# Hyena's inverse transforms turned round: the table stationary, 256 channels moving, results with times on partitions

## The chip, the cores and the metric

One core of a Trainium2 chip. The time is the device time of one execution in microseconds; the kernel before was run three times, and the median counts. The trace comes from one more execution, which was profiled.

## What is computed

One layer of an encoder block over 512 tokens of 2048 features: a norm, a wide input projection, two branches (hyena, 1024 channels, and mlstm, four heads), a gated merge, and a feed-forward part of 5632 hidden units. The change lies in hyena: for each channel, two long convolutions by FFT of length 1024, each with a bias term, between three short-convolved inputs hv, hx1, hx2.

```python
filt = hyena_filters(L, ...)                      # (512, order, 2, 1024)
kf = two_sided_spectrum(filt)                     # h_fwd, one zero, h_bwd reversed without its time 0
z = hx1 * long_conv(hv, kf[:, 0], hb[0])
y_a = hx2 * long_conv(z, kf[:, 1], hb[1])

def long_conv(u, kf, bias):
    uf = jnp.fft.rfft(u, n=2 * L, axis=1)
    y = jnp.fft.irfft(uf * kf[None], n=2 * L, axis=1)[:, :L]
    return y + u * bias
```

## The kernel before

**Numbers.** Every large product is made of three float32r matmuls (`mm3`, L72): each operand is split into a high part, a cast on ScalarE, and a low part, a subtraction on VectorE (`gsplit` L316 with its operations at L319 and L320, `split_w` L165 with L169 and L170). `mm` is L70, so all of these matmuls carry that line; in the trace the moving operand is named first and the stationary one second. Small products in plain fp32 also go through `mm`.

**Main work and side work.** The input projection (`w_in_cols`, L1064) is the main generator. Each of its ticks is two blocks of contraction: 12 matmuls of 512 columns, or 24 of 256 for mlstm's v; there are 220 ticks. `Weights.get` (L180) emits the load (L162, SyncE's queue, three raw buffers) and the split of weights two units ahead of their use. In between, `drive` (L247) lets the side work go on: each tick gives it a budget of 2.2, and every `yield` of a side generator takes its cost from that. The side is two streams that take turns (`turns`, L900): one makes the filters' spectra, the other runs hyena for four groups q of 256 channels and mlstm for four heads, in the order hyena 0 and 1, mlstm 0, hyena 2 and 3, mlstm 1 to 3. A `yield "pause"` holds a stream back for two ticks; `need` waits for a result of the other. What is left of the side when the projection ends would run alone. Behind both comes the merge (a Winograd form, L985 on).

**Hyena for one q** (`hyena`, L743, `conv_long`, L680). Two tiles of u, each 128 channels by 512 times, are loaded by GpSimd's queue (L756 is the load of the gating tile x1 or x2). Times stand in four classes (every fourth time). Eight TensorE transposes (L688) into two PSUM tiles put times on the partitions, and `gsplit` splits them. The forward transform has the DFT table stationary (dH, dL) and 256 channels moving (`sums`, L576). The spectrum is multiplied with the filter's on VectorE and four sums of it are split (A). The inverse transform (L735 on) has the spectrum stationary, 128 channels of it, and 128 columns of the table moving; its result has channels on the partitions again. `finish` (L759) adds bias times u and multiplies by x1 (L764, into z) or by x2 (L768, which also reorders the times, and a store to d_ya, L769). For the second order z goes through transposes and split as u did.

**The filter's spectrum** (`spectrum`, L622). w3 comes by SyncE's queue, the window by GpSimd's (L633). Forward and backward filters are added and subtracted, so that at time 0 the sum holds the backward filter's first value too, which the reference leaves out. Two fp32 matmuls of w3 with `h2["c"]` (one column) give that value with channels on the partitions, and `hbias2` (L640) is the bias less that value.

**Buffers.** All tiles from `gt` and `vt` share 24 buffers (`NG`, L298), those of `sg` nine, the PSUM tiles of `sd_ps` four banks.

Of the kernel before, what the change touches and what calls it, by code (L numbers as in the profile page):

```python
# [9 lines left out]
F32R = mybir.dt.float32r  # L10
AF = mybir.ActivationFunctionType
# [4 lines left out]
P = 128  # L16
# [18 lines left out]
def hybrid_block_kernel(ctx, tc, x, norm1_w, w_in, conv_w, conv_b, filt_w1, filt_b1, filt_freq1,  # L35
# [6 lines left out]
    def new(pool, tag, shape=(P, L), dt=F32):  # L42
        n_tile[0] += 1
        return pool.tile(list(shape), dt, tag=tag, name=f"{tag}_{n_tile[0]}")
# [21 lines left out]
    def sd_ps():  # L66
        return new(psd, "sd")

    def mm(o, a, b, start, stop):
        nc.tensor.matmul(o, a, b, start=start, stop=stop)  # L70
# [20 lines left out]
    sel32 = csm[0:32, 3 * P:3 * P + 16]  # L91
    onesf = new(cp, "onesf", (P, P))
    nc.vector.memset(onesf, 1.0)
    onesr = new(cp, "onesr", (P, P), F32R)
    nc.vector.tensor_copy(onesr, onesf)

    xp_cm = tc.tile_pool(name="xp", bufs=1)
    xp = xp_cm.__enter__()
    rows_a = new(xp, "rows_a", (120, P))
    nc.scalar.dma_start(rows_a, conv_w[0].rearrange("k (b p) -> (k b) p", p=P))  # L100
    rows_b = new(xp, "rows_b", (88, P))
    nc.scalar.dma_start(rows_b[0:40], conv_b[0].rearrange("(b p) -> b p", p=P))
    nc.scalar.dma_start(rows_b[40:56], norm1_w[0].rearrange("(b p) -> b p", p=P))
    nc.scalar.dma_start(rows_b[56:72], norm2_w[0].rearrange("(b p) -> b p", p=P))
    nc.scalar.dma_start(rows_b[72:88], hyena_bias[0].rearrange("o (b p) -> (o b) p", p=P))
    cols = new(cp, "cols", (P, 208))
    pt = sd_ps()
    nc.tensor.transpose(pt[:, 0:120], rows_a, ident[0:120, 0:120])
    nc.tensor.transpose(pt[:, 120:208], rows_b, ident[0:88, 0:88])
    nc.vector.tensor_copy(cols, pt[:, 0:208])  # L110
    cw = cols[:, 0:120].rearrange("p (k b) -> p k b", k=3)
    cb = cols[:, 120:160]
    n1 = cols[:, 160:176]
    n2 = cols[:, 176:192]
    hbias = cols[:, 192:208]
    hbias2 = new(cp, "hbias2", (P, 16))


    def dram(name, shape=(P, L)):
# [188 lines left out]
    def sg(dt=F32, shape=(P, L)):  # L308
        n_tile[0] += 1
        return ph.tile(list(shape), dt, tag="sg", name=f"sg_{n_tile[0]}", bufs=9)  # L310
# [5 lines left out]
    def gsplit(src, shape=(P, L)):  # L316
        h = gt(F32R, shape)
        l = gt(F32R, shape)
        nc.scalar.copy(h, src)  # L319
        nc.vector.tensor_tensor(l, src, h.bitcast(F32), ALU.subtract)  # L320
        return h, l
# [192 lines left out]
    def filter_net():  # L514
        for m in range(4):
            t = gt()
            nc.gpsimd.dma_start(t, c_dft[m])
            hh = new(ph, f"dH{m}", dt=F32R)
            ll = new(ph, f"dL{m}", dt=F32R)
            nc.scalar.copy(hh, t)  # L520
            nc.vector.tensor_tensor(ll, t, hh.bitcast(F32), ALU.subtract)
            dft.append((hh, ll))
            yield 1
        vec = new(ph, "fvec", (P, 4))
        for j, src in enumerate((filt_b1, filt_freq1, filt_b2, filt_freq2)):
            for half in range(2):
                nc.gpsimd.dma_start(vec[half * 64:half * 64 + 64, j:j + 1], src[0].rearrange("(n o) -> n o", o=1))
        w1 = new(ph, "fw1", (33, 2, 64))
        w2 = new(ph, "fw2", (64, 2, 64))
        for half in range(2):  # L530
            nc.gpsimd.dma_start(w1[:, half, :], filt_w1[0])
            nc.gpsimd.dma_start(w2[:, half, :], filt_w2[0])
        zt = gt()
        nc.gpsimd.dma_start(zt[0:33], c_zt)

        def sin_layer(ps, b, fr):
            a = gt()
# [12 lines left out]
        yield 4  # L550
        h1 = sin_layer(ps, vec[:, 0:1], vec[:, 1:2])
        ps = sd_ps()
        mm(ps, w2.rearrange("p a b -> p (a b)"), h1[0:64], True, True)
        yield 4
        hh = sin_layer(ps, vec[:, 2:3], vec[:, 3:4])
        h2["H"] = new(ph, "h2H", dt=F32R)
        h2["L"] = new(ph, "h2L", dt=F32R)
        nc.scalar.copy(h2["H"], hh)
        nc.vector.tensor_tensor(h2["L"], hh, h2["H"].bitcast(F32), ALU.subtract)
        h2["c"] = new(ph, "h2c", (64, 1))  # L560
        nc.vector.tensor_copy(h2["c"], hh[0:64, 0:1])
        yield 4


# [57 lines left out]
    def spectrum(q, o):  # L622
# [8 lines left out]
        for b in range(2):  # L631
            t = gt(shape=(P, 2, 256))
            nc.gpsimd.dma_start(t, c_win[b * 256:(b + 1) * 256, c0:c0 + 256].rearrange("(b p) c -> p b c", p=P))  # L633
            wt.append(t)
        yield .1
        ps = sd_ps()
        for j in range(2):
            mm(ps[:, j:j + 1], w3[0:64, 256 + j * P:256 + (j + 1) * P], h2["c"], True, True)
        ci = o * 8 + 2 * q
        nc.vector.tensor_tensor(hbias2[:, ci:ci + 2], hbias[:, ci:ci + 2], ps[:, 0:2], ALU.subtract)  # L640
        wpm = gt()
        nc.vector.tensor_tensor(wpm[:, 0:256], w3[:, 0:256], w3[:, 256:512], ALU.add)
        nc.vector.tensor_tensor(wpm[:, 256:512], w3[:, 0:256], w3[:, 256:512], ALU.subtract)
# [6 lines left out]
        for tb in range(4):  # L650
            ts = slice(tb * P, (tb + 1) * P)
            ps = sd_ps()
            mm(ps, h2["H"][:, ts], stk, True, False)
            mm(ps, h2["L"][0:64, ts], stk[0:64], False, True)
            pq = gt()
            wv = wt[tb // 2][:, tb % 2:tb % 2 + 1, :].to_broadcast([P, 2, 256])
            nc.vector.tensor_tensor(pq.rearrange("p (j c) -> p j c", j=2), ps.rearrange("p (j c) -> p j c", j=2),
                                    wv, ALU.mult)
            h, l = sg(F32R), sg(F32R)
            nc.scalar.copy(h, pq)  # L660
            nc.vector.tensor_tensor(l, pq, h.bitcast(F32), ALU.subtract)
            PQ.append((h, l))
            yield 1.3
# [13 lines left out]
                yield "wait"  # L677
            yield from spectrum(n // 2, n % 2)

    def conv_long(q, o, u, finish):  # L680

        src = []
        for half in range(2):
            ps = sd_ps()
            for b in range(2):
                for j in range(2):
                    tc0 = half * 256 + b * P
                    nc.tensor.transpose(ps[:, b * 256 + j * P:b * 256 + (j + 1) * P], u[j][:, tc0:tc0 + P], ident)  # L688
            h, l = gsplit(ps)
            for b in range(2):  # L690
                src.append((h[:, b * 256:(b + 1) * 256], l[:, b * 256:(b + 1) * 256]))
            yield .6
        yield "pause"
        yield from need(("spec", q, o))
        U = []
# [33 lines left out]
                yield 1.2  # L729
        yield "pause"  # L730
        where = ((A[0], A[1]), (A[2], A[2]), (A[1], A[0]), (A[3], A[3]))
        for j in range(2):
            ps = sd_ps()
            for c in range(4):
                for sine in range(2):  # L735
                    yH, yL = where[c][sine]
                    dH, dL = table(1, c, sine)
                    cs = slice(sine * 256 + j * P, sine * 256 + (j + 1) * P)
                    mm3(ps[:, c * P:(c + 1) * P], yH[:, cs], yL[:, cs], dH, dL, sine == 0, sine == 1)
            finish(j, ps)  # L740
            yield 1.2

    def hyena(q):  # L743
        yield from need(("hy", q))
        u = []
        for j in range(2):
            t = gt()
            nc.gpsimd.dma_start(t, d_hy[0][2 * q + j])
            u.append(t)
        yield .1  # L750
        for o in range(2):
            nu = []
            xg = []
            for j in range(2):
                t = gt()
                nc.gpsimd.dma_start(t, d_hy[1 + o][2 * q + j])  # L756
                xg.append(t)

            def finish(j, ps):  # L759
                ci = o * 8 + 2 * q + j  # L760
                t = gt()
                nc.vector.scalar_tensor_tensor(t, u[j], hbias2[:, ci:ci + 1], ps, ALU.mult, ALU.add)
                if o == 0:
                    nc.vector.tensor_tensor(t, t, xg[j], ALU.mult)  # L764
                    nu.append(t)
                else:
                    y = gt()
                    nc.vector.tensor_tensor(natural(y), classes(t), classes(xg[j]), ALU.mult)  # L768
                    nc.gpsimd.dma_start(d_ya[2 * q + j], y)  # L769

            yield from conv_long(q, o, u, finish)
            u = nu
            yield "pause"


    def mlstm(h):
# [689 lines left out]
```

## Time and profile before

| | |
|---|---|
| median of 3 runs | 2948.95 us (2946.33 to 2950.16) |
| the profiled execution's own time | 2950.35 us |
| its span (first to last instruction) | 2948.6 us |
| TensorE busy, instructions | 2904.2 us, 18604 |
| VectorE busy, instructions | 2120.0 us, 3853 |
| ScalarE busy, instructions | 1259.9 us, 2234 |
| GpSimd busy, instructions | 187.7 us, 433 |

PE is TensorE's matmuls, PEld its loads of the stationary operand, DVE VectorE, ACT ScalarE, POOL GpSimd, SPq SyncE's DMA queue. A row names line, engine, operation, output and inputs by tile, shape and count, then busy time and mean duration of one, then the engine's idle time just before and what ended it. Busy time is that of a group's union, so overlapping matmuls count once, and the mean is one instruction's own duration, from start to modelled end. How far instructions follow each other is read from the timeline: start, duration, name, and how many were merged in the row.

### The profile page before, as it was taken

To read this page: it belongs to the slowest core of one execution; us is meant where nothing else is said; L and a number is where in the kernel's file an instruction comes from. 1 tells how busy PE (TensorE), PEld (TensorE's weight loads), DVE (VectorE), ACT (ScalarE), POOL (GpSimd) and SP (SyncE) were. 2 spreads that over 40 slices of the span, in tenths; PEclk is the share of its full clock that TensorE was granted. 3 is DMA by queue.
4 is the path that set the end of the run, shared out by engine and by line. 5 is a ranking of instruction groups with operands and counts; after the bars stand their busy time and mean duration, and the time that the engine had idled before them with its cause. 6 is when DMAs were issued, how large, how long until landed. Compare 5 with 4: busy or idle time off the path is not lost.

```text
span 2948.6 us, 48562 instructions
## 1 busy us (share of the span) xinstructions
PE 2904.2 (98%) x18604; PEld 2622.0 (89%) x18604; DVE 2120.0 (72%) x3853; ACT 1259.9 (43%) x2234; POOL 187.7 (6%) x433
## 2 busy tenths in 40 slices
PE   8999999999999999999999999999999999999998
PEld 6788887898779999888899999999999998888886
DVE  6889878878459888645447888888888885233336
ACT  5334343436535554423344444444444444333224
POOL 1001110101100000100010000000000000000000
PEclk9999999999999999999999999999999999999999
DMA  5333343333434444833444333343333436334433
GB/s 175 108 111 113 112 133 101 122 115 120 145 122 132 134 126 129 271 125 108 134 130 136 112 119 122 115 128 117 119 119 115 125 99 215 100 119 124 126 110 128
DMA packets 285201, 377.02 MB, mean 128 GB/s; under 512 B 18021, under 2 KB 221163, under 8 KB 284969
## 3 DMA queue, kind: packets, MB, share of 16 engines
q1 hardware_dynamic: 261264, 301.18, 33.2%
q0 software_dynamic: 22272, 70.55, 7.0%
q8 instruction: 145, 2.38, 0.3%
q10 hardware_dynamic: 1433, 2.20, 0.2%
q14 instruction: 87, 0.71, 0.1%
HBM read 326.67 MB, written 47.20 MB: 127 GB/s over the span
## 4 chain that ended last, share of the span: by engine, by line
PE 66%; issue 2%; DMA 2%; DVE 1%; ACT 0%; POOL 0%; SPq 0%; POOLq 0%; DVEq 0%; ACTq 0%
PE mm L70 46%; PE sd L70 20%; DMA wr<-in_w_down_dram 1%; DMA bt<-d_o 1%; PE sd L1225 0%; DMA d_o<-st 0%; DVE h L81 0%; DMA bt<-d_ya 0%; DVE T L1253 0%; DVE l L977 0%; DVE wl L170 0%; DVE s L993 0%; ACT h L80 0%; POOL d_o L390 0%; DVE x L1365 0%
## 5 line engine op out<-in xcount | busy, mean ns | idle before, releaser
L170 DVE TENSOR_TENSOR wl<-wr,wh 128x512 fp32r<-128x512 f32 x512 | 350.5, 689 | 489.1 <-ACT wh L169 483.7
L169 ACT CAST wh<-wr 128x512 fp32r<-128x512 f32 x512 | 316.4, 621 | 766.5 <-PE mm L70 725.7
L70 PE MATMUL mm<-a,wh 128*128 128x512 f32 (+1 forms) x2136 | 625.7, 376 | 0.9 <-ACT wh L169 0.8
L70 PE MATMUL mm<-T,h 128*128 128x256 f32 x2592 | 466.0, 282 | 3.9 <-ACT h L976 3.9
L70 PE MATMUL sd<-T,h 128*128 128x256 f32 x2592 | 463.8, 282 | 0.0
L70 PEld LDWEIGHTS mm<-a,wh 128*128 128x128 f32 x2136 | 387.0, 189 | 70.1 <-issue 2.6
L70 PEld LDWEIGHTS mm<-T,h 128*128 128x128 f32 x2592 | 400.6, 190 | 4.4 <-ACT h L976 4.4
L70 PE MATMUL mm<-a,wl 128*128 128x512 f32 (+1 forms) x1068 | 399.4, 375 | 3.4 <-DVE wl L170 3.3
L70 PEld LDWEIGHTS sd<-T,h 128*128 128x128 f32 x2592 | 399.4, 189 | 0.0
L70 PE MATMUL mm<-wh,h 128*128 128x512 f32 x1280 | 395.6, 390 | 3.0 <-ACT h L80 3.0
L70 PE MATMUL mm<-T,l 128*128 128x256 f32 x1296 | 366.0, 283 | 0.8 <-DVE l L977 0.8
L70 PE MATMUL sd<-T,l 128*128 128x256 f32 x1296 | 365.2, 282 | 0.0
L976 ACT CAST h<-s 128x512 fp32r<-128x512 f32 x395 | 244.5, 620 | 280.9 <-PE sd L70 138.3
L70 PEld LDWEIGHTS mm<-wh,h 128*128 128x128 f32 x1280 | 241.1, 188 | 53.5 <-ACT h L80 3.2
L977 DVE TENSOR_TENSOR l<-s,h 128x512 fp32r<-128x512 f32 x395 | 270.6, 686 | 11.6 <-ACT h L976 9.2
L976 ACT CAST h<-r 128x512 fp32r<-128x512 f32 x285 | 176.6, 620 | 217.9 <-PE mm L70 108.1
L70 PE MATMUL mm<-wh,a 128*128 128x256 f32 (+1 forms) x1152 | 260.2, 319 | 0.0
L70 PE MATMUL mm<-wl,h 128*128 128x512 f32 x640 | 249.3, 390 | 0.0
L70 PEld LDWEIGHTS mm<-T,l 128*128 128x128 f32 x1296 | 245.0, 189 | 1.2 <-DVE l L977 1.2
L70 PEld LDWEIGHTS sd<-T,l 128*128 128x128 f32 x1296 | 244.3, 189 | 0.0
L70 PEld LDWEIGHTS mm<-a,wl 128*128 128x128 f32 x1068 | 201.8, 189 | 40.7 <-DVE wl L170 5.9
L977 DVE TENSOR_TENSOR l<-r,h 128x512 fp32r<-128x512 f32 x285 | 192.4, 688 | 54.0 <-ACT h L976 47.1
(373 smaller groups left out, 4432.7 us busy)
## 6 DMA issues: line engine op xcount, KB each, us to landing
r<-in_w_gate_up_dram SPq DMA_DIRECT2D x176, 512.0 KB, 4.0
wr<-in_w_in_dram SPq DMA_DIRECT2D x144, 512.0 KB, 3.9
wr<-in_w_down_dram SPq DMA_DIRECT2D x88, 512.0 KB, 3.7
r<-in_w_in_dram SPq DMA_DIRECT2D x32, 512.0 KB, 4.6
wr<-in_w_out_dram SPq DMA_DIRECT2D x32, 512.0 KB, 3.7
d_h<-xo POOLq DMA_DIRECT2D x44, 256.0 KB, 2.6
hl<-d_h SPq DMA_DIRECT2D x44, 256.0 KB, 3.6
d_g<-xo POOLq DMA_DIRECT2D x32, 256.0 KB, 4.2
```

The costliest lines, as they stand in the source:

```text
L70: nc.tensor.matmul(o, a, b, start=start, stop=stop)
L169: nc.scalar.copy(h, src)
L170: nc.vector.tensor_tensor(l, src, h.bitcast(F32), ALU.subtract)
L976: nc.scalar.copy(h, a)
L977: nc.vector.tensor_tensor(l, a, h.bitcast(F32), ALU.subtract)
```

## The change

The inverse transform is turned round: the table is stationary and the 256 channels of a q move, so that a result holds two blocks of 128 times by 256 channels and times stand on the partitions. What was done with channels on partitions moves accordingly:

- `conv_long` no longer transposes; it takes split halves with times on partitions. Per q, `hyena` transposes u (8), x1 (8, then copied to SBUF by ScalarE) and the final result (8); z is made with times on partitions and needs no transposes.
- The gate of order 0 is one multiplication from PSUM and the split; the result of order 1 is copied out by ScalarE (`keep`), transposed, and multiplied by x2 in the natural order of times straight from PSUM.
- x1 is loaded together with u and transposed behind it; x2 is loaded after the first convolution.
- The bias is a constant at time 0 of the filter. Its row is loaded per spectrum (SyncE's queue, one partition, 256 values, a buffer of the shared ring), scaled on ScalarE by 2^-9 as the window is, and VectorE puts half of sum plus difference, which is the forward filter alone, plus the bias into row 0 of the sum. `hbias2`, `h2["c"]`, their matmuls and the bias rows in the constants' transposes go; so does `onesr`, which nothing used.
- Costs of yields: the two inverse halves 1.4 each (1.2 before), 1.1 for each final tile, none for the transposes of z; one pause more per q.

```diff
@@ spectrum
+        row = gt()
+        nc.sync.dma_start(row[0:1, 0:256], hyena_bias[0][o:o + 1, c0:c0 + 256])
         yield .1
-        ps = sd_ps()
-        for j in range(2):
-            mm(ps[:, j:j + 1], w3[0:64, 256 + j * P:256 + (j + 1) * P], h2["c"], True, True)
-        ci = o * 8 + 2 * q
-        nc.vector.tensor_tensor(hbias2[:, ci:ci + 2], hbias[:, ci:ci + 2], ps[:, 0:2], ALU.subtract)
...
+            if tb == 0:
+                nc.scalar.activation(row[0:1, 0:256], row[0:1, 0:256], AF.Copy, scale=2.0 ** -9)
+                nc.vector.tensor_tensor(row[0:1, 256:512], pq[0:1, 0:256], pq[0:1, 256:512], ALU.add)
+                nc.vector.scalar_tensor_tensor(pq[0:1, 0:256], row[0:1, 256:512], 0.5, row[0:1, 0:256],
+                                               ALU.mult, ALU.add)
@@ conv_long
-    def conv_long(q, o, u, finish):
-        src = []
+    def by_times(u):
         for half in range(2):
             ps = sd_ps()
             for b in range(2):
                 for j in range(2):
                     tc0 = half * 256 + b * P
                     nc.tensor.transpose(ps[:, b * 256 + j * P:b * 256 + (j + 1) * P], u[j][:, tc0:tc0 + P], ident)
-            h, l = gsplit(ps)
+            yield ps
+
+    def conv_long(q, o, halves, finish):
+        src = []
+        for h, l in halves:
             for b in range(2):
                 src.append((h[:, b * 256:(b + 1) * 256], l[:, b * 256:(b + 1) * 256]))
-            yield .6
         yield "pause"
...
-        for j in range(2):
-            ps = sd_ps()
-            for c in range(4):
-                for sine in range(2):
-                    yH, yL = where[c][sine]
-                    dH, dL = table(1, c, sine)
-                    cs = slice(sine * 256 + j * P, sine * 256 + (j + 1) * P)
-                    mm3(ps[:, c * P:(c + 1) * P], yH[:, cs], yL[:, cs], dH, dL, sine == 0, sine == 1)
-            finish(j, ps)
-            yield 1.2
+        for half in range(2):
+            ps = sd_ps()
+            for b in range(2):
+                for sine in range(2):
+                    yH, yL = where[2 * half + b][sine]
+                    dH, dL = table(1, 2 * half + b, sine)
+                    cs = slice(sine * 256, sine * 256 + 256)
+                    mm3(ps[:, b * 256:(b + 1) * 256], dH, dL, yH[:, cs], yL[:, cs], sine == 0, sine == 1)
+            finish(half, ps)
+            yield 1.4
@@ hyena (new body, after need)
+        u = load(0)
+        x1 = load(1)
+        yield .1
+        halves = []
+        for ps in by_times(u):
+            halves.append(gsplit(ps))
+            yield .6
+        x1t = []
+        for ps in by_times(x1):
+            t = gt()
+            nc.scalar.copy(t, ps)
+            x1t.append(t)
+        yield "pause"
+        z = []
+        def gate(half, ps):
+            t = x1t[half]
+            nc.vector.tensor_tensor(t, ps, t, ALU.mult)
+            z.append(gsplit(t))
+        yield from conv_long(q, 0, halves, gate)
+        x2 = load(2)
+        y = []
+        def keep(half, ps):
+            t = gt()
+            nc.scalar.copy(t, ps)
+            y.append(t)
+        yield "pause"
+        yield from conv_long(q, 1, z, keep)
+        yield "pause"
+        for j in range(2):
+            ps = sd_ps()
+            for c in range(4):
+                c0 = (c % 2) * 256 + j * P
+                nc.tensor.transpose(ps[:, c * P:(c + 1) * P], y[c // 2][:, c0:c0 + P], ident)
+            t = gt()
+            nc.vector.tensor_tensor(natural(t), classes(ps), classes(x2[j]), ALU.mult)
+            nc.gpsimd.dma_start(d_ya[2 * q + j], t)
+            yield 1.1
```

## Rows read from the trace of the kernel before

**Rows 1.** The page: busy time of the engines over the span, and VectorE's busy tenths in 40 equal slices of the span.

```profile
PE 2904.2 (98%) x18604; PEld 2622.0 (89%) x18604; DVE 2120.0 (72%) x3853; ACT 1259.9 (43%) x2234; POOL 187.7 (6%) x433
...
DVE  6889878878459888645447888888888885233336
```

**Rows 2.** The table of windows, the hyena stage: window, its length, busy us (and instructions) of PE, PEld, DVE, ACT, POOL, granted clock, DMA share, GB/s.

```profile
123.00:664.00 541.00, 535.59 (x3025) 456.54 (x3025) 449.11 (x825) 208.25 (x354) 58.00 (x159) 1.00 0.38 117
```

**Rows 3.** The waits of PE in the same stretch: who waited for whom, us in total, times, the longest.

```profile
PE mm L70 <- DVE wl L170: 3.0, 3, 1.9
PE sd L688 <- DMA g<-d_hy: 1.5, 1, 1.5
```

**Rows 4.** Groups of ScalarE's instructions by line and shape in the same stretch.

```profile
L169 ACT CAST wh<-wr 128x512 fp32r<-128x512 f32 x140 | 86.7, 620 | 209.3 <-PE mm L70 192.2 <-issue 7.9 <-DVE g L715 3.3
...
L587 ACT COPY g<-sd 128x512 f32<-128x512 f32 x23 | 13.5, 587 | 11.5 <-PE sd L70 9.5 <-DVE g L590 1.7
```

**Rows 5.** The waits of SyncE's DMA queue over the first 900 us (L783 loads mlstm's tiles into the shared buffers).

```profile
SPq L162 <- DVE wl L170: 703.6, 102, 17.7
...
SPq L783 <- DMA d_yb<-g: 1.2, 1, 1.2
```

**Rows 6.** PE's timeline, half of an inverse transform (24 matmuls, the first and the last of 17 rows) and what follows it.

```profile
185.54 0.22 PE L70 MATMUL sd<-dH,g 128*128 128x128 f32 x1
...
188.17 0.45 PE L70 MATMUL sd<-g,h2H 128*128 128x512 f32 x1
```

**Rows 7.** Groups of PE's instructions by line and shape, whole span: the inverse transforms, the transposes of u and z, and the products with h2["c"].

```profile
L70 PE MATMUL sd<-dH,g 128*128 128x128 f32 x256 | 45.1, 274 | 0.0
...
L70 PE MATMUL sd<-dL,g 128*128 128x128 f32 x128 | 35.1, 274 | 0.0
...
L688 PE MATMUL sd<-csm,g 128*128 128x128 f32 x64 | 9.3, 273 | 1.5 <-DMA g<-d_hy 1.5
...
L70 PE MATMUL sd<-h2c,sg 64*128 64x1 f32 x32 | 4.8, 252 | 0.0
```

**Rows 8.** PE's timeline, a forward transform's products (24 matmuls, the first two and the last of 16 rows) and what follows.

```profile
506.20 0.40 PE L70 MATMUL sd<-g,dH 128*128 128x256 f32 x2
506.43 0.28 PE L70 MATMUL sd<-g,dL 128*128 128x256 f32 x1
...
508.94 0.28 PE L70 MATMUL sd<-g,dL 128*128 128x256 f32 x1
509.05 0.63 PE L70 MATMUL mm<-a,wh 128*128 128x512 f32 x2
```

**Rows 9.** PE's timeline around the products with h2["c"] of one spectrum.

```profile
234.51 0.62 PE L70 MATMUL mm<-a,wh 128*128 128x512 f32 x2
234.97 0.39 PE L70 MATMUL mm<-a,wl 128*128 128x512 f32 x1
235.28 0.60 PE L70 MATMUL sd<-h2c,sg 64*128 64x1 f32 x4
235.82 0.72 PE L70 MATMUL mm<-a,wh 128*128 128x512 f32 x2
236.38 0.40 PE L70 MATMUL mm<-a,wl 128*128 128x512 f32 x1
```

**Rows 10.** PE's timeline around eight transposes of hyena.

```profile
614.75 0.39 PE L70 MATMUL mm<-a,wl 128*128 128x512 f32 x1
614.98 1.03 PE L688 MATMUL sd<-csm,g 128*128 128x128 f32 x8
615.77 0.71 PE L70 MATMUL mm<-a,wh 128*128 128x512 f32 x2
616.32 0.39 PE L70 MATMUL mm<-a,wl 128*128 128x512 f32 x1
```

**Rows 11.** PE's timeline around the last work of the side streams, eight transposes of mlstm.

```profile
827.57 0.39 PE L70 MATMUL mm<-a,wl 128*128 128x512 f32 x1
827.88 1.09 PE L869 MATMUL sd<-csm,g 128*128 128x128 f32 x8
828.73 0.71 PE L70 MATMUL mm<-a,wh 128*128 128x512 f32 x2
```

**Rows 12.** Groups of VectorE's instructions by line and shape from 60 to 870 us.

```profile
L762 DVE SCALAR_TENSOR_TENSOR g<-g,hbias,sd 128x512 f32<-128x512 f32 x16 | 11.9, 746 | 10.3 <-PE sd L70 10.2
...
L768 DVE TENSOR_TENSOR g<-g,g 128x512 f32<-128x512 f32 x8 | 8.6, 1080 | 0.3
...
L643 DVE TENSOR_TENSOR g<-sg 128x256 f32<-128x256 f32 x8 | 3.4, 420 | 0.0
...
L640 DVE TENSOR_TENSOR hbias<-cols,sd 128x2 f32<-128x2 f32 x8 | 1.2, 152 | 0.5 <-PE sd L70 0.5
```

**Rows 13.** The loads of x1 and x2 (L756) on GpSimd's queue: issue in ns (least, median, most), the longest idle time of GpSimd before one and what ended it, and the time to landing.

```profile
L756 POOL DMA_DIRECT2D g<-d_hy x16: 537/544/552, 122.9 to 598.3; - x16
...
  DVE g L657: 13.0, 1
...
DMA to landing us min/median/max: 2.8/3.7/6.7
```

**Rows 14.** The table of windows, two stretches of 20 us in which VectorE is fullest; columns as in rows 2.

```profile
220.00:240.00 20.00, 20.00 (x90) 16.39 (x89) 20.00 (x39) 8.67 (x13) 1.62 (x5) 1.00 0.25 79
...
460.00:480.00 20.00, 16.75 (x67) 12.34 (x67) 19.21 (x34) 7.00 (x12) 2.75 (x8) 0.91 0.49 159
```

**Rows 15.** PE's timeline, the merge's first matmuls.

```profile
874.42 0.40 PE L70 MATMUL mm<-a,wh 128*128 128x256 f32 x2
```

More of the change, by code (lines that the diff above doesn't have):

```diff
@@ L93, in hybrid_block_kernel @@
     nc.vector.memset(onesf, 1.0)
-    onesr = new(cp, "onesr", (P, P), F32R)
-    nc.vector.tensor_copy(onesr, onesf)
     xp_cm = tc.tile_pool(name="xp", bufs=1)
@@ L100, in hybrid_block_kernel @@
     nc.scalar.dma_start(rows_a, conv_w[0].rearrange("k (b p) -> (k b) p", p=P))
-    rows_b = new(xp, "rows_b", (88, P))
+    rows_b = new(xp, "rows_b", (72, P))
     nc.scalar.dma_start(rows_b[0:40], conv_b[0].rearrange("(b p) -> b p", p=P))
@@ L104, in hybrid_block_kernel @@
     nc.scalar.dma_start(rows_b[56:72], norm2_w[0].rearrange("(b p) -> b p", p=P))
-    nc.scalar.dma_start(rows_b[72:88], hyena_bias[0].rearrange("o (b p) -> (o b) p", p=P))
-    cols = new(cp, "cols", (P, 208))
+    cols = new(cp, "cols", (P, 192))
     pt = sd_ps()
     nc.tensor.transpose(pt[:, 0:120], rows_a, ident[0:120, 0:120])
-    nc.tensor.transpose(pt[:, 120:208], rows_b, ident[0:88, 0:88])
-    nc.vector.tensor_copy(cols, pt[:, 0:208])
+    nc.tensor.transpose(pt[:, 120:192], rows_b, ident[0:72, 0:72])
+    nc.vector.tensor_copy(cols, pt[:, 0:192])
     cw = cols[:, 0:120].rearrange("p (k b) -> p k b", k=3)
@@ L114, in hybrid_block_kernel @@
     n2 = cols[:, 176:192]
-    hbias = cols[:, 192:208]
-    hbias2 = new(cp, "hbias2", (P, 16))
     def dram(name, shape=(P, L)):
@@ L559, in filter_net @@
         nc.vector.tensor_tensor(h2["L"], hh, h2["H"].bitcast(F32), ALU.subtract)
-        h2["c"] = new(ph, "h2c", (64, 1))
-        nc.vector.tensor_copy(h2["c"], hh[0:64, 0:1])
         yield 4
@@ L731, in conv_long, with hyena, load @@
         where = ((A[0], A[1]), (A[2], A[2]), (A[1], A[0]), (A[3], A[3]))
+        for half in range(2):
[8 more added lines that the diff above has]
+            yield 1.4
+    def hyena(q):
+        yield from need(("hy", q))
+        def load(kind):
+            ts = []
+            for j in range(2):
+                t = gt()
+                nc.gpsimd.dma_start(t, d_hy[kind][2 * q + j])
+                ts.append(t)
+            return ts
+        u = load(0)
[26 more added lines that the diff above has]
+        yield "pause"
         for j in range(2):
@@ L734, in conv_long @@
             for c in range(4):
-                for sine in range(2):
-                    yH, yL = where[c][sine]
-                    dH, dL = table(1, c, sine)
-                    cs = slice(sine * 256 + j * P, sine * 256 + (j + 1) * P)
-                    mm3(ps[:, c * P:(c + 1) * P], yH[:, cs], yL[:, cs], dH, dL, sine == 0, sine == 1)
-            finish(j, ps)
-            yield 1.2
-    def hyena(q):
-        yield from need(("hy", q))
-        u = []
-        for j in range(2):
-            t = gt()
[L748 to L773, printed above, removed]
+                c0 = (c % 2) * 256 + j * P
+                nc.tensor.transpose(ps[:, c * P:(c + 1) * P], y[c // 2][:, c0:c0 + P], ident)
+            t = gt()
+            nc.vector.tensor_tensor(natural(t), classes(ps), classes(x2[j]), ALU.mult)
+            nc.gpsimd.dma_start(d_ya[2 * q + j], t)
+            yield 1.1
     def mlstm(h):
```

## The prediction

> **What bounds the kernel now.** I read the page first: TensorE is busy 98% of the span, VectorE 72% and at its fullest in the first third [rows 1], and the change touches only the stage there in which the hyena filters run beside the input projection. Then the table of windows: from 123 us (the first hyena channels are loaded) to 664 us (the last are done) TensorE is busy 535.6 of 541 us at full clock, VectorE 449, ScalarE 208 [rows 2]. A busy TensorE may still be a slow one, so I looked at who waits for whom. Of TensorE's 5.4 idle us there, 3.0 are waits for a weight split and 1.5 for a DMA [rows 3]. ScalarE's weight split (L169) waits 192 us for TensorE to give its buffers back [rows 4], and SyncE's weight loads wait 704 us for VectorE's half of the split, the same chain of buffers one step further up [rows 5]. So every feeder is ahead of TensorE. The third look was start to start in the bursts: 24 of the 128-column inverse matmuls take from 185.54 to 188.17 us, 2.63 us, 110 ns each [rows 6], though one is shown as 274 ns [rows 7]; 24 of the 256-column forward matmuls take from 506.20 to 509.05, 2.85 us, 119 ns each [rows 8]; two projection matmuls of 512 columns take 0.46, 0.23 each [rows 9]. Back-to-back spacing, and not the mean duration, is the price of an instruction here. The stage is bound by TensorE's issue, and what is taken off TensorE should come off the time one for one as long as the feeders keep up.
>
> **The inverse transforms.** Before: eight (filter, order) pairs with 2 x 24 matmuls of 128 columns, 384 in all (256 with dH and 128 with dL [rows 7]), 16 bursts x 2.63 = 42.1 us [rows 6]. After: per pair 2 halves x 2 blocks x 2 (cosine, sine) x 3 = 24 matmuls, table stationary, 256 columns moving. That is exactly the shape and operands of the forward burst (table stationary, split data moving), so 8 x 2.85 = 22.8 us [rows 8]. **-19.3 us.** The halved count of loads of the stationary operand is the whole gain; twice the columns cost only 8% more per instruction.
>
> **The correction at time 0.** Before, each spectrum multiplies w3 with h2["c"], two fp32 matmuls of one column, in the trace four records each time, 32 in all [rows 7]. Where the four stand behind a projection matmul, 234.97 to 235.82 us pass, 0.85 instead of 0.23, so they take 0.62; and the two matmuls behind take 0.56 instead of 0.46, 0.10 more: 0.72 us [rows 9]. 8 x 0.72: **-5.8 us.** The same work becomes three instructions on row 0 of tb = 0 (below), none on TensorE.
>
> **The transposes.** Before: u and, between the orders, z, 8 + 8 per q. After: u, x1 and the result, 24 per q; z needs none. So 8 more per q, 32 in all. A block of 8 lies between 614.75 and 615.77: 1.02 less the usual 0.23, plus 0.09 on the next step, 0.88 us [rows 10]; mlstm's block from 827.57 to 828.73 takes 1.02 by the same reckoning [rows 11]. The results are transposed in two blocks of four with other work between, so I add the cost of entering and leaving (about 0.17) once more per q. Bounds 4 x 0.88 = 3.5 and 4 x (1.02 + 0.17) = 4.8; I take **+4.0 us.** The Trainium skill, "TensorE: Matmul & The Clock Gate", Part 4, gives about 275 ns for a transpose in a kernel's context; by that the 32 would cost 8.8 us and the sum below would be 4.8 us smaller. The trace agrees with this as a duration, 273 ns [rows 7], while eight in a row follow each other by 0.10 to 0.11 us [rows 10].
>
> Sum on TensorE: -19.3 - 5.8 + 4.0 = **-21.1 us.**
>
> **VectorE.** Removed: 16 of the 746 ns operation at L762 (11.9 us) and 8 of 152 ns at L640 (1.2). The gate of order 0 stays one 512-wide operation, now from PSUM, as L762 is; the last product stays the 1080 ns of L768, whose output is strided the same; the splits stay eight per q. Added: an add and a combined multiply-add over 256 elements of one partition, for which the nearest row is the 256-wide add at L643, 420 ns, and the multiply-add a little over: 8 x 0.87 = 7.0 [rows 12]. Their bounds are 0.15 us, as L640 with two elements, and 0.75, as L762 with 512: 2.4 to 12 us. Net about -6 us (-11 to -1). All of it lies beside TensorE.
>
> **ScalarE.** Added: 8 copies of x1 and 8 of y from PSUM at the 587 ns of L587, and 8 scalings of 256 elements, at most the same: 9.4 + 4.7 = 14.1 us [rows 4]. 208 of 541 becomes 222; its 192 us of waits for TensorE hide that. Without that slack the 14.1 would stand against the 21.1.
>
> **New waits.** (a) x1 is now transposed right behind u, so TensorE needs the third and fourth load of the group, each issued 0.54 us after the one before on GpSimd's queue; landing takes 3.7 us [rows 13]. In the trace TensorE waited 1.5 us for such a load once [rows 3]. Bounds 0 and 4 x 1.1; I take +1. Behind it on TensorE is the next tick of projection matmuls. (b) The bias row is a new DMA on SyncE's queue into a buffer of the shared ring of 24, ahead of weight loads, on a queue that mostly waits [rows 5]. A block there is the last rival below; I take 0. (c) At tb = 0 VectorE waits for ScalarE's scaled row; behind it stand weight splits. The row is loaded a pause of two ticks earlier, so 0, at most 8 x 0.59 us. (d) VectorE is full in some 20 us windows (20.00 of 20 at 220 us; at 460 us, 19.21, and there TensorE lost 3.25) [rows 14]. With TensorE quicker, such stretches get a little tighter. Bounds -5.4 (all recorded idle of the stage goes) and +8; I take +1.5. (e) At the start, one small DMA and 16 transposed rows fewer, and one copy of ones, all in a stretch that waits for x: 0.
>
> **The pace.** I counted the yields of both streams through `drive` and `turns` by their costs. Before, the side work ends in tick 202 of 220; the trace shows its last transposes done at 828.73 us and projection alone from there to the merge, which begins at 874.42: 45.7 us, 16.6 ticks of 12 matmuls at 0.23 [rows 11, 15], near the 18 of the count. After, per q, the costs rise by 1.8 and there is one pause more, with two pauses falling together twice; the count gives tick 213. Five to seven ticks of cover remain, 14 to 19 us, so this costs nothing; were the cover gone, the overrun would be bare.
>
> Profiled execution: 2950.35 us around a span of 2948.6. 2950.35 - 21.1 + 1 + 1.5 = 2931.8. The median of the three runs is 1.4 us below that execution, so **2930 us.**
>
> **Rivals.** *VectorE becomes a second bound.* Where its windows are full it can't give TensorE its weights any faster; if that holds for half of the stage, half of the 18.6 is lost: 2939. For it: full windows [rows 14] and slices at 8 and 9 tenths [rows 1]. Against: its own load falls by 6 us, and 10.2 us of its idle time are waits for these very inverses at L762 [rows 12]. Chance 0.13. *The 256-column form doesn't gain*, say because a stationary operand that comes back costs more than the forward burst shows, 24 x 0.22 us per pair: only -5.8 + 4.0 and the waits are left, 2950. Against: the forward burst is the same instruction. Chance 0.03. *The side work doesn't end under the projection*: the order of work shifts by more than I count, and the last mlstm units run bare; beyond the five to seven ticks of cover each tick stands bare, at most the 3.84 us that one takes in the stage (541 us over the 141 ticks that the count gives for it). With four such, 2945. Chance 0.04. *SyncE blocks on the row's buffer* (the slower side): the weight loads behind the row come late. The longest such wait on GpSimd's queue was 13.0 us [rows 13]. A weight load may go out three loads, six ticks or 23 us, ahead; landing (as in rows 13) and the two halves of the split at some 0.65 take 5, so a block reaches TensorE only beyond 18 us. With eight blocks of 24 us: +48, 2978. Against: 16 loads into the same ring already stand on this queue for mlstm, and the longest that one of them waited is 1.2 us [rows 5]. Chance 0.04.
>
> **How the numbers follow.** The forecast has 0.76, with its own range of 2922 (all recorded stalls go) to 2938 (full waits at (a) and part of (d)). VectorE as a bound brings the range to 2942. So 2921 to 2942. A measurement of this kernel can tell about 0.2%, 6 us: faster means below 2943. Faster 0.87 (forecast nearly whole, VectorE's rival), same 0.08 (no gain, the small overrun), slower 0.05 (SyncE's block, a longer overrun).
>
> **What would show it.** In the profile after: bursts of 24 inverse matmuls of 256 columns in 2.85 us, no h2c records, 96 transposes of this kind; the merge's begin (874.42 now) earlier by 18 to 21 us, and everything behind it unchanged in length; TensorE's waits in the stage still near 5 us; ScalarE's wait for TensorE at L169 shorter but large; the last mlstm transposes 14 to 19 us before the merge instead of 46. It is wrong if SyncE's waits name the row, if TensorE's waits for weight splits rise by 10 us, or if the stage shortens but a later one grows.

## The result and the profile after

| | median | lowest to highest | runs |
|---|---|---|---|
| before | 2949.77 us | 2946.33 to 2951.93 | 12 |
| after | 2956.61 us | 2951.70 to 2960.61 | 12 |

After / before is 1.0024 (95% interval 1.0015 to 1.0033): 6.8 us slower, where 2930 and faster was predicted. The profiled execution after took 2956.98 us, its span is 2955.0.

Two windows, up to the merge and from it on, say where to look. Columns as in rows 2; first the kernel after:

```profile
0.00:874.26 874.26, 836.67 (x4420) 699.23 (x4421) 662.42 (x1319) 396.70 (x723) 106.88 (x287) 0.99 0.39 122
874.26:2955.00 2080.74, 2057.04 (x13993) 1915.47 (x13991) 1450.11 (x2525) 874.80 (x1536) 78.82 (x146) 1.00 0.41 130
```

The same two windows of the kernel before:

```profile
0.00:874.42 874.42, 854.67 (x4612) 716.15 (x4613) 674.87 (x1338) 385.99 (x703) 108.67 (x287) 0.99 0.39 122
874.42:2948.60 2074.18, 2049.50 (x13993) 1905.88 (x13991) 1445.10 (x2516) 873.92 (x1532) 79.01 (x146) 0.99 0.41 130
```

Up to the merge TensorE has 192 matmul records and 18.0 us of busy time less, and yet the merge begins 0.16 us earlier only: the work went, and idle time took its place (874.26 - 836.67 = 37.6 us against 19.8). And behind the merge, where the change touches nothing, the stretch of the same 13993 matmuls is 6.56 us longer, which is about the whole loss of 6.8 us. So there are two questions: who eats the gain, and what slows a part that wasn't changed.

**The idle time.** Waits of TensorE over the first 900 us, the kernel after (L683 transposes u and x1):

```profile
PE mm L70 <- DVE wl L165: 11.5, 6, 5.4
PE sd L683 <- DMA g<-d_hy: 10.3, 6, 4.5
```

The same of the kernel before:

```profile
PE mm L70 <- DVE wl L170: 3.3, 4, 1.9
PE sd L688 <- DMA g<-d_hy: 1.5, 1, 1.5
```

Two kinds grew, by 8.2 and 8.8 us; the 1.5 us before are those of [rows 3]. The longest wait of the second kind, on GpSimd's queue in the kernel after:

```profile
577.93 0.55 POOL L793 DMA_DIRECT2D d_ya<-g  x1 [5.45 <-DVE wl L165]
578.47 2.13 POOL L750 DMA_DIRECT2D g<-d_hy  x4
```

and on TensorE, same kernel:

```profile
578.88 0.39 PE L70 MATMUL mm<-a,wl 128*128 128x512 f32 x1
583.76 0.44 PE L683 MATMUL sd<-csm,g 128*128 128x128 f32 x1 [4.50 <-DMA g<-d_hy]
```

Here the four loads of u and x1 for the next q (L750) are issued the moment the store of the last q's result (L793) is out, and GpSimd stood idle for 5.45 us in front of that store, waiting for VectorE. TensorE had reached the transposes of those very loads. In the kernel before, `hyena` ended with a pause, so two ticks lay between the store and the next transposes. This meeting costs 4.8 of the 10.3 us. The others are meetings on the same queue, but not all with this store: the loads from 265.62 us on (2.8 us of waits) come behind a store of L793 at 263.80 and stores of the projection, and those from 449.04 us on (1.1 us), where hyena follows mlstm, have mlstm's stores (L893) among them. The first loads of all make TensorE wait for 1.6 us, as they did before (1.5).

All stores of L793 and all 24 loads of L750, those of x2 too, in the kernel after: first the idle time of GpSimd in front of a store until VectorE's product (us, times), then the loads' time from issue to landing:

```profile
  DVE g L792: 38.7, 5
```

```profile
DMA to landing us min/median/max: 2.9/5.1/6.1
```

So GpSimd waits long for the product in front of most stores. The four loads issued at once from 578.47 us on land in 5.2 to 5.7 us; those of x2, two at a time, in 2.9 to 3.6, where [rows 13] have 3.7 in the median. (In front of the store at 577.93 the row names a weight split, L165, which ended last; the product itself, L792, had ended 2.7 us earlier. Why the store stayed for the split, the trace doesn't say.)

**The clock behind a wait.** What such a wait costs besides itself stands in the window from 560 to 600 us, the kernel after:

```profile
560.00:600.00 40.00, 35.16 (x194) 30.63 (x193) 15.70 (x29) 12.47 (x23) 5.40 (x10) 0.91 0.33 106
```

and the kernel before:

```profile
560.00:600.00 40.00, 40.00 (x278) 37.45 (x277) 31.93 (x65) 13.77 (x24) 5.35 (x10) 1.00 0.42 127
```

The granted clock is 0.91 in the mean: for some 7 of these 40 us (40 x 0.09 / 0.5) TensorE ran at 1.2 instead of 2.4 GHz, behind 4.5 us in which it did nothing. In the same stretch before it never stopped, and the clock is 1.00.

By windows of 20 us, TensorE stands at 1.2 GHz for some 20 us ahead of the merge in the kernel after and for some 10 in the kernel before. Two matmuls of 512 columns take 0.85 us at 589.08 us, in the slow stretch, and 0.45 at 577.07, ahead of it. So a microsecond at the lower level costs about half of one, and the difference costs some 5 us (an estimate from these rows). With it the part up to the merge adds up: TensorE's work is 18 + 5 = 23 us less, its idle time 17.8 us more, and the slow clock takes the 5.

**What came as predicted.** One half of an inverse transform, the kernel after (first and last of its eight rows and what follows; [rows 6] show the old form):

```profile
245.21 0.40 PE L70 MATMUL sd<-g,dH 128*128 128x256 f32 x2
...
246.50 0.29 PE L70 MATMUL sd<-g,dL 128*128 128x256 f32 x1
246.63 0.62 PE L70 MATMUL mm<-a,wh 128*128 128x512 f32 x2
```

Groups of TensorE's instructions by line and shape, the kernel after:

```profile
L70 PE MATMUL sd<-g,dH 128*128 128x256 f32 x256 | 47.0, 283 | 0.0
L70 PE MATMUL sd<-g,dL 128*128 128x256 f32 x128 | 35.9, 280 | 0.0
```

Twelve products take 1.42 us, so 24 take 2.84 (2.85 predicted), and forward and inverse transforms together now count 384 such matmuls: the 384 of 128 columns [rows 7] are gone, 192 have come.

### The profile page after: what moved, and what is told of

The parts are those of the page before. It is cut to its first block, busy times and chain, and to the rows that moved or that the text cites. A ratio compares the mean times of both kernels' runs of the same rounds, so it can differ in the third digit from the quotient of the medians.

```text
span 2955.0 us, 48209 instructions
## 1 busy us (share of the span) xinstructions
PE 2893.7 (98%) x18412; PEld 2614.7 (88%) x18412; DVE 2112.5 (71%) x3843; ACT 1271.5 (43%) x2258; POOL 185.7 (6%) x433
## 4 chain that ended last, share of the span: by engine, by line
PE 89%; DVE 4%; DMA 3%; issue 2%; ACT 1%; POOL 0%; SPq 0%; ACTq 0%; DVEq 0%; POOLq 0%
PE mm L70 63%; PE sd L70 25%; DMA wr<-in_w_down_dram 1%; DMA g<-d_hy 1%; DVE wl L165 0%; DMA hl<-d_h 0%; PE sd L683 0%; DMA g<-d_k 0%; DVE st L339 0%; DMA xt<-in_x_dram 0%; DVE st L336 0%; DVE h L81 0%; PE sd L1246 0%; DVE s L1014 0%; DMA g<-d_q 0%
## 5 line engine op out<-in xcount | busy, mean ns | idle before, releaser
L165 DVE TENSOR_TENSOR wl<-wr,wh 128x512 fp32r<-128x512 f32 x512 | 350.3, 689 | 492.9 <-ACT wh L164 485.8
L164 ACT CAST wh<-wr 128x512 fp32r<-128x512 f32 x512 | 315.8, 620 | 763.9 <-PE mm L70 722.1
L998 DVE TENSOR_TENSOR l<-s,h 128x512 fp32r<-128x512 f32 x395 | 270.2, 685 | 11.6 <-ACT h L997 9.0
```

The lines of the kernel that those rows point to most:

```text
L998: nc.vector.tensor_tensor(l, a, h.bitcast(F32), ALU.subtract)
```

## The experiments

Three theories for the missing 27 us: (1) addresses: the change frees 640 bytes per partition of constants (`onesr` 512, `hbias2` 64, 16 columns of `cols` 64), and all buffers allocated behind them move down by that much, the feed-forward part's among them; (2) the loads' place on GpSimd's queue; (3) weight splits late on a VectorE whose work falls together. The rival to all three is that the new inverse itself is dear; the rows above speak against it. Each kernel was run 5 to 11 times. The kernel before measured 2949.49 us (29 runs) beside the first four experiments and 2950.34 (15 runs) beside the last four, so a difference across the two groups can be off by about 0.9 us.

### e1_pad: the old addresses

```diff
     nc.vector.memset(onesf, 1.0)
+    pad = new(cp, "pad", (P, 160))
+    nc.vector.memset(pad[:, 0:1], 0.0)
```

> The changed kernel with 640 bytes per partition of unused tile at the bottom of SBUF, so that every tile behind it lies at the address that it has in the kernel before (the change freed 640 bytes there, and all pools on the left side moved down). Theory 1, addresses set TensorE's pace: in the gate-up stage matmuls follow each other by 118.96 ns in the kernel before and by 120.06 in the changed one, with the same instructions; they go back to 119.0, the stretch from the merge's begin to the end to 2074 us from 2081, and the total falls by 6 to 7 us to about 2950. The first stage keeps its waits. Rival, the slower pace comes from the clock or from chance in one execution: no change by the pad, about 2956.6.

Measured: 2946.31 us (2943.90 to 2952.64), ratio to before 0.9992 (0.9983 to 1.0001); after's interval lies wholly above. A fixed stretch of the feed-forward part, 1580 to 2340 us, in which TensorE never stops, the kernel after:

```profile
1580.00:2340.00 760.00, 760.00 (x6333) 759.77 (x6332) 674.77 (x1183) 359.67 (x606) 20.00 (x37) 1.00 0.38 119
```

and e1_pad:

```profile
1580.00:2340.00 760.00, 759.99 (x6391) 759.70 (x6390) 678.55 (x1193) 363.45 (x613) 20.54 (x38) 1.00 0.39 121
```

The count of matmuls in the same 760 us is the measure: 6333 against 6391 (before: 6392), 120.0 ns each against 118.9, at a granted clock of 1.00, with no wait. 58 matmuls more are 6.9 us. Another part goes the other way: from 1240 to 1360 us after does 531 matmuls of 512 columns and e1_pad 523, as before did. From the merge on, e1_pad:

```profile
873.74:2950.10 2076.36, 2050.29 (x13993) 1905.80 (x13991) 1447.38 (x2524) 875.45 (x1536) 78.82 (x146) 1.00 0.41 130
```

TensorE's busy time there is 6.75 us less than after's; the stretch is 4.4 us shorter, as 2.4 us more of idle time stand in it. The waits ahead of the merge are after's (11.5 and 10.1 us). So theory 1 holds, and it explains the slower tail. The medians differ by 10.3 us, more than these rows account for (the last section takes this up); this profiled run (2951.84) lies at the upper end of e1_pad's.

### e2_load: two ticks between the loads and the transposes

```diff
         x1 = load(1)
         yield .1
+        yield "pause"
         halves = []
...
             x1t.append(t)
-        yield "pause"
         z = []
```

> The changed kernel with the pause that stood behind the transposes of x1 moved to between the loads of u and x1 and the transposes; the count of yields gives the same ticks. Theory 2, a store and the next group's loads stand in one tick on GpSimd's queue: the loads are issued only behind the store's wait for the last product, and TensorE reaches the transposes before they land (10.3 us of waits at L683, three stretches at 269, 457 and 584 us, with clock dips behind them). With two ticks in between the waits fall under 2 us and the merge begins 10 to 14 us earlier, total about 2944. Rival, the loads wait for free buffers of the ring of 24: the waits stay within 3 us of 10.3, total unchanged. Rival, the feeders are the bound: the waits at L683 go, but waits for weight splits on VectorE take their place (11.5 us now, over 18 then), total within 3 us of 2956.6.

Measured: 2945.26 us (2941.73 to 2947.75), ratio 0.9987 (0.9978 to 0.9995). No instruction is added or taken away. Waits over the first 900 us, e2_load:

```profile
PE mm L70 <- DVE wl L165: 11.6, 6, 5.4
PE sd L683 <- DMA g<-d_hy: 2.1, 3, 1.2
```

and its window from 560 to 600 us:

```profile
560.00:600.00 40.00, 38.44 (x209) 32.84 (x208) 27.84 (x54) 14.53 (x24) 4.57 (x12) 1.00 0.32 103
```

8.2 us of waits go, and the clock stays at 1.00 here. Up to the merge, e2_load:

```profile
0.00:858.41 858.41, 829.84 (x4421) 694.73 (x4421) 662.37 (x1319) 396.44 (x723) 107.00 (x287) 1.00 0.40 124
```

The merge begins 15.9 us earlier, about twice the waits that were removed: 9.0 us are idle time, and 6.8 are busy time for the same matmuls. By windows of 20 us TensorE is at 1.2 GHz for some 7 us there instead of some 20, which at half the pace is worth some 6.5 of the 6.8. This profiled run (2941.73) is the fastest of the kernel's runs; in the medians the edit gains 11.3. The tail keeps after's length (2081.59).

### e4_sync: u and x1 on another queue

```diff
-                nc.gpsimd.dma_start(t, d_hy[kind][2 * q + j])
+                (nc.gpsimd if kind == 2 else nc.sync).dma_start(t, d_hy[kind][2 * q + j])
```

> The changed kernel with the loads of u and x1 on SyncE's queue instead of GpSimd's, nothing else. Theory 2 (the loads stand behind a store on GpSimd's queue): the loads go out early, waits at L683 fall from 10.3 to under 3 us, total 2944 to 2948 as long as the weight loads behind them aren't held. Rival, buffers: SyncE waits for buffers of the ring, the weight loads behind come late, and TensorE's waits for weight splits rise over 18 us: total 2960 or more.

Measured: 2944.95 us (2942.59 to 2946.69), ratio 0.9983 (0.9975 to 0.9992). Waits, e4_sync:

```profile
PE mm L70 <- DVE wl L165: 10.6, 6, 5.4
PE sd L683 <- DMA g<-d_hy: 1.1, 1, 1.1
```

The loads stand in the same tick as the transposes, as in after, and only their queue differs. The last four go out by 560.7 us, and the two stores that they stood behind follow on GpSimd's queue at 563.56 and 567.14. Landing is shorter too here (3.8 us in the median, with x2's), so this run alone doesn't part the two; e2_load does, where the same four loads on the old queue land in 4.7 to 5.2 us and TensorE doesn't wait for them. The loads were late because of what stood ahead of them. Theory 2 holds.

### e5_bias: the bias in the filter's row alone

The kernel before, with after's `row` and its three operations at tb = 0 in place of the products with `h2["c"]`, and both gates straight from PSUM; the old inverse and the old addresses stay.

```diff
...
+            if tb == 0:
+                nc.scalar.activation(row[0:1, 0:256], row[0:1, 0:256], AF.Copy, scale=2.0 ** -9)
+                nc.vector.tensor_tensor(row[0:1, 256:512], pq[0:1, 0:256], pq[0:1, 256:512], ALU.add)
+                nc.vector.scalar_tensor_tensor(pq[0:1, 0:256], row[0:1, 256:512], 0.5, row[0:1, 0:256],
+                                               ALU.mult, ALU.add)
...
-                nc.vector.scalar_tensor_tensor(t, u[j], hbias2[:, ci:ci + 1], ps, ALU.mult, ALU.add)
-                if o == 0:
-                    nc.vector.tensor_tensor(t, t, xg[j], ALU.mult)
+                if o == 0:
+                    t = gt()
+                    nc.vector.tensor_tensor(t, ps, xg[j], ALU.mult)
...
-                    nc.vector.tensor_tensor(natural(y), classes(t), classes(xg[j]), ALU.mult)
+                    nc.vector.tensor_tensor(natural(y), classes(ps), classes(xg[j]), ALU.mult)
```

> The kernel before with the bias moved into the filter's row at time 0 and nothing else of the change: the inverse transforms, the transposes and the queues stay as before, the gate reads PSUM directly, and the tiles keep their addresses. It leaves the matmuls with h2[c] out (5.8 us of TensorE by the prediction's step) and 13 us of VectorE, and adds the row's three small operations. If TensorE's issue is the bound and no wait is added: 2950 - 5.8 = 2944, merge at 868.5 instead of 874.4. If a shorter TensorE demand is given back as waits for VectorE in any case: within 2 us of before.

Measured: 2941.95 us (2938.75 to 2943.65), ratio 0.9973 (0.9962 to 0.9984), 7.5 us faster than before. The profile shows only part of that at the place of the edit: the merge begins 3.9 us earlier (870.50), with 6.8 us of waits for weight splits instead of 3.3. TensorE's busy time up to the merge falls by 5.7 us (848.96 from 854.67), where 5.8 were predicted for this part; the row costs nothing that shows. The tail is 3.1 us shorter (2071.10) at the same addresses. That is idle time (20.3 us against 24.7), most of it in waits for splits from the merge on: 5.9 us (L975, L976) against 9.9 before (L976, L977). Why those waits shrank was not tried.

### e3_both: e1_pad and e2_load together

Both diffs above.

> The changed kernel with both edits, the 640 bytes of the pad and the pause between the loads of u and x1 and their transposes. If the two losses are separate (addresses behind the merge, 6.7 us; loads behind stores, 16 us at the merge's begin with the clock dips they cause), they add up: merge at about 858, the rest at 2074 to 2079 us, total about 2936 to 2938. Waits at L683 under 3 us, waits for weight splits still near 11.6 us. Rival: the two share a cause, total not under 2943.

Measured: 2935.72 us (2934.67 to 2937.23), ratio 0.9953 (0.9941 to 0.9966). Adding the two single gains gives 2956.6 - 10.3 - 11.3 = 2935.0, so the two causes add up. What is left above 2930, 5.7 us, is near what the waits for weight splits have above the prediction: 11.6 us, against 3.3 before and 1.5 more allowed.

### e6_onepause: without the pause ahead of the second convolution

```diff
-        yield "pause"
         yield from conv_long(q, 1, z, keep)
```

on e3_both.

> As e3_both, with the pause ahead of the second convolution left out (the convolution begins with one of its own). By the count of yields the order of the side work shifts by two to three ticks in places against the projection's evacuations, and the side ends two ticks earlier. If the 11.6 us of waits for weight splits are coincidences of VectorE's full stretches (evacuation of projection columns, spectrum and mlstm in one tick), they change by several us, the 5.4 us one above all: total 2930 to 2942. If they are VectorE's load as such, they stay at 10 to 13 us and the total within 2 us of e3_both.

Measured: 2929.42 us (2927.29 to 2930.72), ratio 0.9931 (0.9918 to 0.9943), 20.9 us faster than before. Waits over the first 900 us, e6_onepause:

```profile
PE mm L70 <- DVE wl L167: 5.5, 6, 1.9
...
PE sd L685 <- DMA g<-d_hy: 2.6, 2, 2.3
```

Its two windows, up to the merge and from it on:

```profile
0.00:852.71 852.71, 829.66 (x4421) 694.68 (x4421) 665.39 (x1329) 395.01 (x726) 106.26 (x287) 1.00 0.40 125
852.71:2927.60 2074.89, 2050.57 (x13993) 1906.14 (x13991) 1445.16 (x2516) 875.11 (x1533) 78.80 (x146) 1.00 0.41 130
```

The merge begins 21.7 us earlier than before; behind it all is as long as before within 0.7 us; against e3_both the waits for weight splits fell by 6.1 us and the time by 6.3. (Other waits rose a little; the idle time up to the merge fell by 4.2 in all.) This is the time that was predicted, 0.6 us below the range expected for this run, but on a kernel with three edits that the predicted one doesn't have. It is the best one measured.

### e7_ahead3: weights split three units ahead

```diff
-    AHEAD = 2
+    AHEAD = 3
```

on e3_both.

> As e3_both, with the weights of the projection split three units ahead instead of two, in the same four buffers. Theory 3: what is left of the gap to the prediction are stretches in which VectorE's backlog (up to 11 us) is longer than the two ticks (7.7 us) by which the split is ahead; three ticks cover most of it: waits for weight splits 11.6 to under 5 us, total 5 us or more below e3_both. Rival: with all four buffers ahead, ScalarE waits for TensorE to free one at each split and holds its copies for the side work: TensorE's waits on ScalarE rise and the total is not lower.

Measured: 2933.54 us (2929.17 to 2937.80), ratio 0.9940 (0.9926 to 0.9953). Waits over the first 900 us, e7_ahead3:

```profile
PE sd L685 <- DMA g<-d_hy: 4.1, 2, 3.2
...
PE mm L70 <- DVE pp L334: 2.6, 1, 2.6
PE mm L70 <- DVE wl L167: 1.9, 2, 1.6
```

The waits for splits go from 11.6 to 1.9 us, and the median falls by 2.2 only, inside the spread of the runs: others have come, for the loads (4.1) and for the projection's evacuation (L334, 2.6). (This profiled run, 2937.80, is the slowest of the five.) The 5 us expected didn't come. The late splits can be bought off, but VectorE's work then comes late elsewhere. Whether this kernel gains at all over e3_both is left open.

### e8_pad256: another address, neither old nor after's

```diff
-    pad = new(cp, "pad", (P, 160))
+    pad = new(cp, "pad", (P, 64))
```

on e3_both: 256 bytes instead of 640.

> As e3_both, with a pad of 256 instead of 640 bytes. If TensorE's pace in the gate-up stage hangs on where the stationary tiles lie against the moving ones, the mean spacing differs from both 118.96 (as before) and 120.0 (without pad) or falls on one of them, and the stretch behind the merge follows it by 6.4 us per ns; the first stage stays as in e3_both. If only the exact layout of the kernel before is quick, it is 120.0 and the total about 2943 to 2945.

Measured: 2944.58 us (2941.82 to 2948.34), ratio 0.9981 (0.9972 to 0.9990), 8.9 us slower than e3_both. The window of the feed-forward part, e8_pad256:

```profile
1580.00:2340.00 760.00, 760.00 (x6336) 760.00 (x6335) 672.22 (x1170) 358.60 (x604) 20.60 (x38) 1.00 0.38 119
```

6336, near after's 6333; its merge begins as early as e3_both's (857.52 against 858.30), so the whole loss lies behind it: 2084.3 us to the end of the span at 2941.8, against e3_both's 2075.6. The two kernels differ in the size of the pad alone. Some padding doesn't help; of the three shifts tried only the one that restores the old addresses is quick here.

## Why the prediction was wrong, step by step

**The sum on TensorE (-21.1 us) was right to within some 2 us.** The inverse and the 256-column form came at the spacings read from the bursts. Up to the merge the work fell by 23 us in the kernel after by the reckoning above, and in e6_onepause TensorE's busy time fell by 25.0 us (829.66 from 854.67), some 1.5 of it from the clock. That e6_onepause begins the merge 21.7 us earlier, close to the sum, is this less 3.3 us more of idle time. The rival that the 256-column form gains nothing is out. What failed are the terms that stood beside the sum.

**(a), the new waits for x1, was mis-sized and misread.** I priced how late the third and fourth load land behind the first (1 us taken, 4.4 the upper bound). The waits went from 1.5 to 10.3 us, 8.8 more, and taking them away is worth 10.6 to 11.3 us of time (e1_pad to e3_both, after to e2_load), the slow clock behind them included. What I looked at were the transposes that moved; what counts is everything on the queue ahead of their loads. With the trailing pause gone, the store of one q stands right ahead of the loads of the next wherever two q follow each other, and it waits for a product that itself needs the last transposes. The place to look was the order on GpSimd's queue, not the landing time of a load. The Trainium skill, "DMA: Bandwidth & Descriptors", section "Anatomy of one DMA — SWDGE (gpsimd) path", states that a wait for a semaphore is held by the issuing sequencer ahead of dispatch, not by the DMA engines; the rows at 577.93 and 578.47 us agree: 5.45 us of idle in front of the store and the four loads right behind it.

**The clock was no term of the sum.** It was put at nothing without a reason, though [rows 14] have a stop of 3.25 us with a clock of 0.91 beside it: the prediction prices where TensorE stops, not what its clock does behind a stop. It took some 5 us up to the merge.

**"Everything behind it unchanged in length" was wrong by 6.56 us.** I never priced what freed constants do: they move the addresses of every later buffer. It is 10.3 us of the median by e1_pad, 9.5 by e2_load to e3_both, 8.9 by e8_pad256, some 7 of it the matmuls' pace (last section). A later stage that grows was one of the prediction's own signs of being wrong.

**(d), VectorE's full stretches, was mis-sized:** +1.5 taken, +8 the upper bound, 8.2 us measured in waits (11.5 against 3.3). VectorE's total did fall, as predicted, but the costs of the yields and the pauses decide what falls together. The longest such wait, TensorE in the kernel after, lies where the sums for the merge's input (L954 to L971, the filter stream's last work), the projection's evacuation (L336, L342) and a split meet:

```profile
726.96 0.58 PE L70 MATMUL mm<-wl,a 128*128 128x256 f32 x1 [5.45 <-DVE wl L165]
```

VectorE's timeline of the same moment:

```profile
723.89 0.41 DVE L971 TENSOR_TENSOR T<-g,T 128x256 fp32r<-128x256 f32 x1
724.23 0.74 DVE L336 SCALAR_TENSOR_TENSOR st<-pp,cols,st 128x512 f32<-128x512 f32 x1
724.89 0.75 DVE L971 TENSOR_TENSOR T<-g,T 128x256 fp32r<-128x256 f32 x2
725.56 0.74 DVE L342 SCALAR_TENSOR_TENSOR st<-pp,cols,st 128x512 f32<-128x512 f32 x1
726.22 0.68 DVE L165 TENSOR_TENSOR wl<-wr,wh 128x512 fp32r<-128x512 f32 x1
```

The split that TensorE waits for comes directly behind other work, with no gap. One pause less took 6.1 us of these waits and 6.3 us of time. It moves other work too, so that the pause's place is the cause is shown, and which of the meetings it undoes is not. The rival that VectorE becomes a second bound had the right engine, but its price was half of the whole gain, and the stage isn't bound by VectorE: e6_onepause has the same VectorE work and all of the gain.

**Right, or nearly:** (b), the row's load (L629) held SyncE's queue once, for 0.2 us; and (c), ScalarE waited once for the row, 0.7 us. ScalarE's added work is hidden, its wait for TensorE at L169 (L164 after) is still there, 196.5 us where it was 192.2 [rows 4] and a shorter one was forecast. VectorE's added operations, the kernel after, against 420 ns and a little over estimated:

```profile
L653 DVE SCALAR_TENSOR_TENSOR g<-g 1x256 f32<-1x256 f32 x8 | 3.2, 403 | 0.0
...
L652 DVE TENSOR_TENSOR g<-g 1x256 f32<-1x256 f32 x8 | 3.2, 403 | 0.0
```

One partition of 256 elements takes 403 ns, 128 partitions took 420 (L643 [rows 12]). **The pace** was off: the last mlstm transposes end at 866.67 us, 7.6 us ahead of the merge instead of 14 to 19. The side work still ended under cover.

By the steps after, e1_pad, e3_both, e6_onepause the medians go 2956.61, 2946.31, 2935.72, 2929.42: 10.3 us for addresses, 10.6 for the queue, 6.3 for the second pause. By the prediction's terms, in profiled spans: 2930.0 was forecast and 2955.0 came. 7.8 us are (a) above its 1, 6.7 are (d) above its 1.5, some 5 the clock and 6.6 the tail, and some 2 go off for the greater saving; that is 24 of the 25.

## What to carry to other kernels

When a step is moved, write down for each of its loads what stands ahead of it on its queue and what that waits for: a store at the end of one round holds back the loads of the next, and a pause between them may be all that hid it. When a change frees or adds a constant, compare a stage that it doesn't touch by the count of matmuls in one fixed window, and hold the addresses with a pad while the change itself is judged. A sum of spacings read from bursts gives the work well; the waits have to be priced from the order in which things now meet.

## What was not expected of the hardware

Matmuls of 256 columns in fully busy stretches follow each other every 118.9 or 120.0 ns by where their buffers lie (6391 or 6333 in 760 us at a clock of 1.00), and in the stage of 512 columns the same shift goes the other way (523 or 531 in 120 us). The Trainium skill, "SBUF — State Buffer", section "Operand start alignment", speaks of which start addresses are legal and says that its runs timed nothing; the runs here show that among legal ones the pace differs by 0.9%. Why is open: no run tells whether it is the stationary or the moving operand, or another engine's access to the same memory. In the profiles the cause is of one size: TensorE's busy time behind the merge differs by 6.75 us (after to e1_pad), 6.3 (e2_load to e3_both) and 6.6 (e8_pad256 to e3_both), while the stretch itself, with its idle time, differs by 4.4, 6.0 and 8.7. That the medians differ by 9 to 10 us lies in part at the clock: over all runs the mean granted clock is 0.9929 in after and 0.9935 in e1_pad, 0.9937 in e2_load and 0.9946 in e3_both, 0.9942 in e8_pad256. Multiplied by it, the mean spans differ by 7.1, 6.9 and 7.6 us (an estimate from the listed clocks). Why the slower kernels were granted less is open.
